# Row-summed modulation coefficients, a reordered opening and eight first feature tiles in a SwiGLU block kernel

## The chip, the cores and the metric

The kernel runs on one core of one Trainium2 chip. The metric is the device time of one execution in microseconds (us), from the first to the last instruction with what the launch puts around them; smaller is better. Five engines work side by side, each through its own instructions in order: TensorE (PE, with its weight loads listed as PEld), VectorE (DVE), ScalarE (ACT), GpSimd (POOL) and SyncE (SP), which here issues the loads.

## The reference, cut to what matters

The whole model is three blocks for 256 tokens of width 1024: a block with two SwiGLU layers and two attentions side by side, then two attention and MLP blocks. The change touches how the first block's modulation is made, and the beginning of its first SwiGLU:

```python
mods = (silu(c) @ w_ada + b_ada).reshape(B, 9, 1024)      # shift, scale, gate for 3 sublayers
n = rmsnorm(h, g_pre[i]) * (1 + scale(i)) + shift(i)
f = (silu(n @ w_gate) * (n @ w_up)) @ w_down              # 1024 -> 2816 -> 1024
h = h + 0.5 * gate(i) * rmsnorm(f, g_post[i])
```

`c` is one vector of 1024 numbers and `w_ada` is 1024 x 9216, so the nine modulation vectors are nine matrix-vector products of 1024 x 1024 each; chunk j of the kernel is the j-th of them (0, 3, 6 shifts; 1, 4, 7 scales; 2, 5, 8 gates).

## The kernel before, in words

All matrix work is done in fp32 split into two parts: a weight tile `raw` of 128 x 1024 is loaded, ACT copies it into a rounded high part `wh` (L489), DVE subtracts to get the low part `wl` (L495, now and then POOL), and TensorE adds three products: high by high, high by low, low by high. The activations are split the same way into `nh` and `nl`.

One list, `plan()`, gives the order of all pieces of the weight stream. `pump_one` takes the next piece: it issues loads up to seven pieces ahead on SP's queue (L435), and puts the split, or for a modulation piece the sum, on ACT and DVE. `pump` keeps a set number of split weights ahead of TensorE. Each engine runs its instructions in the order in which Python wrote them. Small side jobs (`bg`) are generators that `tick` moves one step on after each weight.

The opening (`start_ffn`): x is normed and transposed by TensorE into `yT` (features on partitions). Then comes a loop over the eight k-tiles of the 1024 input features. Before k can be used, `n[0][:, k]` and `n[1][:, k]` need the shift and scale of those 128 features. The piece for them (`ad0`) holds 128 columns of the shift and 128 of the scale; ACT and DVE scale its eight row blocks by silu(c) and add them up (L448, L450: 128 x 256 each, one on ACT and seven on DVE), TensorE sums over the partitions with a column of ones (`reduce_`, 4 instructions), two small DVE operations add the bias and the gain (L1019, L1020), ACT makes `y2` and `nh` (L1023, L1024), DVE makes `nl` (L1028). Then `first(k, 0)` and `first(k, 1)` put the gate and up products of feature tiles 0 to 6 (M0 = 7) into seven PSUM banks, 21 matmuls each (three passes over seven tiles). The eighth bank serves the reductions.

After the loop, seven `swiglu` calls (ACT Silu L914, DVE product L915, ACT and DVE split L918, L919) empty the banks, while TensorE goes on with feature tile 7 in the free bank (`ffn_steps`: 24 matmuls for gate, 24 for up), and from then on with up and down tiles.

The modulation chunks 2 to 8 are spread as pieces over the later stream. A chunk of eight pieces (128 rows x 1024 columns) is summed over row blocks by DVE (L458 for the first piece of a shift or scale, L460 for the others, and with `bz`, a tile with the bias in its first row, for the first piece of a gate). Then `ada_columns` (shifts and scales; 16 TensorE instructions with a column of ones) or `ada_gate` finishes the chunk.

Of the kernel before, what the change touches and what calls it, by code (L numbers as in the profile page):

```python
# [10 lines left out]
F32 = mybir.dt.float32  # L11
# [7 lines left out]
P = 128  # L19
S = 256  # L20
# [41 lines left out]
M0 = 7  # L62
# [45 lines left out]
def plan():  # L108
# [23 lines left out]
    for k in range(2):  # L132
        out += [(("ad0", k, 0), 1024), (("ad0", k, 1), 1024)]
        if k == 0:
            out.append((("s0", 0, 0), M0 * P))
    for k in range(8):
        out.append((("s0", k, 1), M0 * P))
        if k < 6:
            out += [(("ad0", k + 2, 0), 1024), (("ad0", k + 2, 1), 1024)]
        if k < 7:  # L140
            out.append((("s0", k + 1, 0), M0 * P))
# [54 lines left out]
def pack_stream(a):  # L196
# [11 lines left out]
    def piece(key):  # L208
        n = key[0]
        if n == "ad0":  # L210
            _, k, q = key
            w = a["w_ada"][0][512 * q:512 * q + 512]
            w = np.concatenate([w[:, P * k:P * k + P], w[:, D + P * k:D + P * k + P]], axis=1)
        elif n == "s0":
# [5 lines left out]
        elif n == "ada":  # L220
            _, j, k = key
            w = a["w_ada"][0][P * k:P * k + P, 1024 * j:1024 * j + 1024]
# [99 lines left out]
def model_kernel(ctx, tc, x, stream, cols, const, rows, bada, relb, onehot, out):  # L322
# [71 lines left out]
    for i in range(2):  # L394
        nc.sync.dma_start(h[1][:, 512 * i:512 * i + 512], x[tk(1), 512 * i:512 * i + 512])
# [16 lines left out]
    bz = cp.tile([P, D], F32, name="bz")  # L412
    pool.memset(bz, 0.0)
    nc.sync.dma_start(bz[0:1, :], bada[2:3, :])
# [15 lines left out]
    ada_end = {}  # L430
    bg = []

    def load(key, n, off):
        raw = w1k("raw0") if key[0] == "ad0" else rawp.tile([P, RAWC], F32, tag="raw", name="raw")
        nc.sync.dma_start(raw[:, 0:n], stream[off:off + P * n].rearrange("(p w) -> p w", p=P))  # L435
        return raw[:, 0:n]

    def ada_item(key, raw):
        if key[0] == "ad0":
            _, k, q = key  # L440
            if q == 0:
                ada_acc["a"] = w256("ada")
            a = ada_acc["a"]
            for j in range(4):
                c = sc[:, 4 * q + j:4 * q + j + 1]
                r = raw[:, j * 2 * P:(j + 1) * 2 * P]
                if q == 0 and j == 0:
                    act.activation(a, r, AF.Copy, scale=c)  # L448
                else:
                    dve.scalar_tensor_tensor(a, r, c, a, op0=ALU.mult, op1=ALU.add)  # L450
            return
        _, j, k = key
        if k == 0:
            ada_acc[j] = w1k("ada")
        a = ada_acc[j]
        c = sc[:, k:k + 1]
        if k == 0 and j % 3 < 2:
            dve.tensor_scalar(a, raw, c, None, op0=ALU.mult)  # L458
        else:
            dve.scalar_tensor_tensor(a, raw, c, a if k else bz, op0=ALU.mult, op1=ALU.add)  # L460
        if k == 1 and j in (2, 5):
            nc.sync.dma_start(bz[0:1, :], bada[j + 3:j + 4, :])
        if k == 7:
            bg.append(ada_end[j](j, a))
            if j == 4:
                st["lo"] = "dve"
# [3 lines left out]
    def pump_one():  # L470
# [7 lines left out]
        if key[0] in ("ada", "ad0"):  # L478
# [25 lines left out]
    def pump(ahead=None):  # L504
        ahead = st["ahead"] if ahead is None else ahead
        while st["i"] < len(items):
            if items[st["i"]][0][0] not in ("ada", "ad0") and st["w"] >= st["rel"] + ahead + extra():
# [356 lines left out]
    bp1 = cp.tile([P, 72], F32, name="bp1")  # L864
    G = {}

    def ada_columns(j, a):
        for _ in range(4 if j == 3 else 2):
            yield
        ps = bank()  # L870
        for k in range(8):
            mm(ps[:, 2 * k:2 * k + 1], a[:, k * P:(k + 1) * P], ones[:, 0:1], start=(k == 0))
        v = ps.rearrange("p (k two) -> p k two", two=2)[:, 0:8, 0]
        i, sh = j // 3, j % 3 == 0
        if sh:
            dve.tensor_tensor(ac_b[:, i, :], v, cl[:, C_BADA + 8 * j:C_BADA + 8 * j + 8], op=ALU.add)
        else:
            tmp = small(8)
            dve.tensor_tensor(tmp, v, bp1[:, 8 * j:8 * j + 8], op=ALU.add)
            dve.tensor_tensor(ac_a[:, i, :], tmp, cl[:, C_GPRE + 8 * i:C_GPRE + 8 * i + 8], op=ALU.mult)  # L880
# [23 lines left out]

    for j in (3, 4, 6, 7):
        ada_end[j] = ada_columns
    for j in (2, 5, 8):
        ada_end[j] = ada_gate
# [69 lines left out]
    def start_ffn():  # L978
# [3 lines left out]
        dve.tensor_scalar(bp1, cl[:, C_BADA:C_BADA + 72], 1.0, None, op0=ALU.add)  # L982
        ss = [small(2) for _ in range(2)]
        for t in range(2):
            for hf in range(2):
                square_sum(half(t, hf), D, ss[t][:, hf:hf + 1])
        tps = []
        for t in range(2):
            r = inv_rms(ss[t])
            ys = [w512("y") for _ in range(2)]  # L990
            for hf in range(2):
                if t:
                    act.activation(ys[hf], half(t, hf), AF.Copy, scale=r)
                else:
                    dve.tensor_scalar(ys[hf], half(t, hf), r, None, op0=ALU.mult)
            tps += [transposes(ys[hf], 4) for hf in range(2)]
        pump_one()
        pump_one()
        for i, tp in enumerate(tps):
# [971 lines left out]
```

## Time and profile before

| what | us |
|---|---|
| median of 3 runs | 1164.33 (1160.9 to 1165.6) |
| the profiled execution, its own time | 1167.6 |
| its span, first to last instruction | 1165.8 |
| PE busy | 1120.3 |
| DVE busy | 746.2 |
| ACT busy | 603.4 |

The mean granted clock of TensorE in the profiled execution is 0.99. How to read it: an engine's busy time is the union of its instructions, a row of the timeline is a start, a length, the engine, the line, what is written from what, and in brackets how long the engine had been idle and what released it. Matmuls overlap, so the step from one start to the next is the price of one, not its length.

### The profile page before, as it was taken

What the parts mean: (1) busy time and instruction counts of PE and PEld (TensorE: products, weight loads), DVE (VectorE), ACT (ScalarE), POOL (GpSimd) and SP (SyncE); (2) the same over time, 40 slices, a digit from 0 to 9 for tenths busy, and PEclk for the clock granted to TensorE, in tenths of its full rate; (3) what the DMA queues carried; (4) which work ended last, traced back from release to release, by engine and by line L of the source; (5) the groups of instructions that cost most, each with busy time, mean ns of one, the idle gap of its engine ahead of it and who ended that gap; (6) DMA issues with size and microseconds to landing.
All of it is one profiled execution on the core that took longest, in us unless ns stands there. A gap on an engine that the chain in (4) does not pass through costs nothing.

```text
span 1165.8 us, 18854 instructions
## 1 busy us (share of the span) xinstructions
PE 1120.3 (96%) x7268; PEld 1012.5 (87%) x7268; DVE 746.2 (64%) x1286; ACT 603.4 (52%) x1159; POOL 144.4 (12%) x152
## 2 busy tenths in 40 slices
PE   5999999899999899999999799999999999999997
PEld 5998999799888799999887678999998888999996
DVE  5987866689667776455656657555566746655554
ACT  5564444554576544343564566444457655544443
POOL 1001000204000300000058630000003200000001
PEclk9999999999999999999999999999999999999999
DMA  8978977468447385545544234655544523755540
GB/s 289 352 265 318 374 291 244 139 217 325 162 148 250 142 308 190 205 168 184 178 158 149 89 124 143 210 193 188 191 152 140 199 92 126 251 182 184 194 148 37
DMA packets 65920, 230.27 MB, mean 198 GB/s; under 512 B 7275, under 2 KB 8691, under 8 KB 65702
## 3 DMA queue, kind: packets, MB, share of 16 engines
q1 hardware_dynamic: 63798, 225.07, 55.8%
q10 hardware_dynamic: 1776, 3.29, 0.8%
q8 instruction: 57, 0.93, 0.3%
q0 software_dynamic: 256, 0.71, 0.2%
q14 instruction: 33, 0.27, 0.1%
HBM read 227.98 MB, written 2.63 MB: 198 GB/s over the span
## 4 chain that ended last, share of the span: by engine, by line
PE 76%; DVE 10%; ACT 7%; issue 3%; POOL 3%; DMA 0%; SPq 0%; POOLq 0%; ACTq 0%; DVEq 0%
PE mm L547 39%; PE acc L547 35%; DVE wl L495 2%; ACT wh L489 2%; POOL wl L495 2%; PE mm L632 1%; DVE ada L450 1%; DVE ada L460 1%; ACT junk L607 1%; ACT s L1491 1%; POOL sm L604 1%; ACT s L1346 1%; DVE s L1569 0%; DMA h<-in_x_dram 0%; DVE y L701 0%
## 5 line engine op out<-in xcount | busy, mean ns | idle before, releaser
L495 DVE TENSOR_TENSOR wl<-raw,wh 128x1024 fp32r<-128x1024 f32 (+4 forms) x318 | 380.4, 1210 | 86.5 <-ACT wh L489 86.4
L489 ACT ACTIVATE wh<-raw 128x1024 fp32r<-128x1024 f32 (+3 forms) x350 | 354.7, 1034 | 14.0 <-DMA raw<-in_stream_dram 12.9
L547 PE MATMUL mm<-nl,wh 128*128 128x256 f32 x1128 | 314.6, 284 | 0.0
L547 PE MATMUL mm<-nh,wh 128*128 128x256 f32 x1128 | 314.4, 284 | 0.0
L547 PE MATMUL mm<-nh,wl 128*128 128x256 f32 x1128 | 314.3, 283 | 0.0
L547 PEld LDWEIGHTS mm<-nl,wh 128*128 128x128 f32 x1128 | 214.5, 192 | 3.0
L547 PEld LDWEIGHTS mm<-nh,wh 128*128 128x128 f32 x1128 | 214.5, 192 | 3.0
L547 PEld LDWEIGHTS mm<-nh,wl 128*128 128x128 f32 x1128 | 214.2, 192 | 0.0
L547 PE MATMUL acc<-wl,fh 128*128 128x512 f32 x372 | 120.4, 390 | 1.5 <-DVE wl L495 1.5
L547 PE MATMUL acc<-wh,fh 128*128 128x512 f32 x372 | 120.9, 392 | 0.0
L547 PE MATMUL acc<-wh,fl 128*128 128x512 f32 x372 | 119.7, 389 | 0.0
L1089 ACT ACTIVATE rl<-mm 128x256 f32<-128x256 f32 x64 | 24.6, 384 | 160.9 <-PE mm L547 160.9
L495 POOL TENSOR_TENSOR wl<-raw,wh 128x512 fp32r<-128x512 f32 (+2 forms) x64 | 81.7, 1305 | 203.1 <-ACT wh L489 203.1
L604 POOL TENSOR_TENSOR sm<-sm,nhalf 128x1 f32<-128x1 f32 (+1 forms) x36 | 21.5, 597 | 631.4 <-DVE sm L613 566.9
L1090 DVE TENSOR_TENSOR ff<-rl 128x256 f32<-128x256 f32 x64 | 27.2, 425 | 102.5 <-ACT rl L1089 102.5
L914 ACT ACTIVATE sg<-mm 128x256 f32<-128x256 f32 x38 | 14.4, 382 | 137.8 <-PE mm L547 137.8
L547 PEld LDWEIGHTS acc<-wl,fh 128*128 128x128 f32 x372 | 69.9, 188 | 18.1 <-DVE wl L495 3.2
L547 PEld LDWEIGHTS acc<-wh,fl 128*128 128x128 f32 x372 | 69.9, 188 | 14.8
L547 PE MATMUL acc<-wh,nh 128*128 128x512 f32 (+3 forms) x208 | 79.2, 404 | 1.1 <-ACT nh L637 1.1
L547 PE MATMUL acc<-wh,nl 128*128 128x512 f32 (+3 forms) x208 | 75.3, 386 | 0.6 <-DVE nl L638 0.6
L547 PE MATMUL acc<-wl,nh 128*128 128x512 f32 (+3 forms) x208 | 75.1, 385 | 0.0
L547 PEld LDWEIGHTS acc<-wh,fh 128*128 128x128 f32 x372 | 65.5, 189 | 9.1
(322 smaller groups left out, 1638.3 us busy)
## 6 DMA issues: line engine op xcount, KB each, us to landing
raw<-in_stream_dram SPq DMA_DIRECT2D x395, 512.0 KB, 4.6
raw<-in_stream_dram SPq DMA_DIRECT2D x16, 448.0 KB, 6.5
raw<-in_stream_dram SPq DMA_DIRECT2D x8, 384.0 KB, 3.4
raw<-in_stream_dram SPq DMA_DIRECT2D x8, 292.0 KB, 3.2
gp<-in_rows_dram SPq DMA_DIRECT2D x3, 512.0 KB, 6.6
wide<-scr ACTq DMA_DIRECT2D x1, 1536.0 KB, 9.3
raw<-in_stream_dram SPq DMA_DIRECT2D x4, 320.0 KB, 3.0
h<-in_x_dram SPq DMA_DIRECT2D x4, 256.0 KB, 3.6
```

Of the source, the lines that this page charges most:

```text
L450: dve.scalar_tensor_tensor(a, r, c, a, op0=ALU.mult, op1=ALU.add)
L460: dve.scalar_tensor_tensor(a, raw, c, a if k else bz, op0=ALU.mult, op1=ALU.add)
L489: act.activation(wh[:, 0:n], raw, AF.Copy)
L495: e.tensor_tensor(wl[:, u:v], raw[:, u:v], wh[:, u:v].bitcast(F32), op=ALU.subtract)
L547: pe.matmul(o, l, r, start=start, stop=True, skip_group_check=True)
L604: pool.tensor_tensor(o, v, nhalf[:, 0:v.shape[-1]], op=ALU.pow)
L607: act.activation(junk(p_.shape[-1]), p_, AF.Square, scale=1.0 / math.sqrt(n) if scale is None else scale, accum_out=acc_)
L632: pe.transpose(tp[:, j * P:(j + 1) * P], src[:, j * P:(j + 1) * P], ident)
L914: act.activation(sg, ps[:, 0:S], AF.Silu)
L1089: act.activation(rl, ps[:, 0:S], AF.Relu)
L1090: dve.tensor_tensor(ff, rl, rl, op=ALU.mult)
L1346: act.activation(s[:, c], s[:, c], AF.Exp, bias=nm[:, t:t + 1], accum_out=rsum[:, 2 * t + j:2 * t + j + 1])
```

## The change

Shifts and scales (chunks 0, 1, 3, 4, 6, 7) come transposed in the stream: a piece now holds 128 output features on the partitions and all 1024 inputs along the row. silu(c) is spread over all partitions once (`cb`, by eight TensorE instructions against the identity and two ACT operations), and one DVE operation for each piece multiplies and sums along the row, with bias and gain as its scalars, and leaves a finished coefficient column. The TensorE reductions with ones, `ada_columns` and the small DVE operations behind them are gone. Gates keep their sum over row blocks, but their bias now comes in as eight 128 x 128 ACT copies of the identity scaled by the bias; the tile `bz`, its memset and its three small loads are gone.

In the opening, the second half of x is loaded behind the first modulation piece, its squares are summed by DVE, the coefficients for k = 0 are applied straight from PSUM, and the first group of matmuls runs in two halves of four banks. M0 is 8: eight feature tiles run in the k loop, on all eight PSUM banks, and `ffn_steps` starts at tile 8.

```diff
-M0 = 7
+M0 = 8
...
     def ada_item(key, raw):
...
+        if j % 3 < 2:
+            dst, init, scale = (ac_b, cl[:, C_BADA + 8 * j + k:C_BADA + 8 * j + k + 1], 1.0) if j % 3 == 0 else \
+                (ac_a, bpg[:, 8 * i + k:8 * i + k + 1], cl[:, C_GPRE + 8 * i + k:C_GPRE + 8 * i + k + 1])
+            dve.tensor_tensor_reduce(out=raw, in0=raw, in1=cb, scale=scale, scalar=init, op0=ALU.mult, op1=ALU.add,
+                                     accum_out=dst[:, i, k:k + 1])
         else:
-            dve.scalar_tensor_tensor(a, raw, c, a if k else bz, op0=ALU.mult, op1=ALU.add)
...
+            if k == 0:
+                ada_acc[j] = w1k("ada")
+                for m in range(8):
+                    act.activation(ada_acc[j][:, m * P:(m + 1) * P], ident, AF.Copy,
+                                   scale=cl[:, C_BADA + 8 * j + m:C_BADA + 8 * j + m + 1])
+            a = ada_acc[j]
+            dve.scalar_tensor_tensor(a, raw, sc[:, k:k + 1], a, op0=ALU.mult, op1=ALU.add)
...
+        cps = [bank() for _ in range(2)]
+        for k in range(8):
+            mm(cps[k // 4][:, k % 4 * P:k % 4 * P + P], cl[:, C_C + k:C_C + k + 1].broadcast_to([P, P]), ident,
+               start=(k % 4 == 0))
+        raws.append(load(*items[0]))
+        for i in range(2):
+            nc.sync.dma_start(h[1][:, 512 * i:512 * i + 512], x[tk(1), 512 * i:512 * i + 512])
...
+        for i in range(2):
+            act.activation(cb[:, 512 * i:512 * i + 512], cps[i], AF.Silu)
...
+        for hf in range(2):
+            dve.tensor_tensor_reduce(out=ys[1][hf], in0=half(1, hf), in1=half(1, hf), scale=1.0 / D, scalar=0.0,
+                                     op0=ALU.mult, op1=ALU.add, accum_out=ss[1][:, hf:hf + 1])
...
         def coefficients(k):
-            ps = red[0]
...
+            src = yT[:, k, :] if k else tps[0][:, 0:S]
+            a, b = ac_a[:, 0, k:k + 1], ac_b[:, 0, k:k + 1]
+            act.activation(n[0][:, k, :], src, AF.Identity, scale=a, bias=b)
             y2 = w256("y2")
+            act.activation(y2, src, AF.Identity, scale=a, bias=b)
...
+            if k == 0 and q == 0:
+                groups = [((passes[0], passes[2], passes[1]), ms) for ms in (range(4), range(4, M0))]
...
         for k in range(8):
             pump_one()
             first(k, 0)
             if k < 7:
-                reduce_(k + 1)
```

## Rows read from the trace of the kernel before

**Rows 1.** The page: busy time of the engines, share of the span, instructions.
```profile
PE 1120.3 (96%) x7268; PEld 1012.5 (87%) x7268; DVE 746.2 (64%) x1286; ACT 603.4 (52%) x1159; POOL 144.4 (12%) x152
```

**Rows 2.** Timeline of the start: start us, length us, engine, instruction, [idle before, releaser].
```profile
7.87 0.63 ACT L607 ACTIVATE junk<-h 128x512 bf16<-128x512 f32 x1 [1.04 <-DMA h<-in_x_dram]
...
9.51 1.33 ACT L993 ACTIVATE y<-h,sm 128x512 f32<-128x512 f32 x2 [0.92 <-POOL sm L604]
...
11.27 3.68 DVE L450 SCALAR_TENSOR_TENSOR ada<-raw,sc,ada 128x256 f32<-128x256 f32 x7 [2.43 <-ACT ada L448]
...
18.44 1.23 PE L547 MATMUL acc<-nh,wh 128*128 128x256 f32 x4 [2.36 <-ACT wh L489]
```

**Rows 3.** Timeline of VectorE through one turn of the k loop.
```profile
31.38 0.21 DVE L1020 SCALAR_TENSOR_TENSOR ac_a<-mm,bp,cl 128x1 f32<-128x1 f32 x1
...
33.46 0.42 DVE L1028 TENSOR_TENSOR nl<-y,nh 128x256 fp32r<-128x256 f32 x1
...
33.79 2.09 DVE L495 TENSOR_TENSOR wl<-raw,wh 128x896 fp32r<-128x896 f32 x2
...
35.80 1.52 DVE L450 SCALAR_TENSOR_TENSOR ada<-raw,sc,ada 128x256 f32<-128x256 f32 x3
...
37.30 0.21 DVE L1020 SCALAR_TENSOR_TENSOR ac_a<-mm,bp,cl 128x1 f32<-128x1 f32 x1
```

**Rows 4.** Windows of the opening: busy (count) per engine, granted clock, DMA share, GB/s.
```profile
20.00:25.00 5.00, 5.00 (x25) 4.91 (x25) 4.75 (x10) 0.03 (x1) 0.00 (x0) 1.00 0.64 211
25.00:30.00 5.00, 5.00 (x34) 5.00 (x34) 4.89 (x11) 3.10 (x5) 0.00 (x0) 1.00 0.93 337
30.00:35.00 5.00, 5.00 (x44) 4.97 (x43) 4.82 (x12) 3.10 (x5) 0.00 (x0) 1.00 1.02 392
```

**Rows 5.** Timeline where the opening ends: first swiglu, tile 7, first down tile.
```profile
67.84 0.66 ACT L914 ACTIVATE sg<-mm 128x256 f32<-128x256 f32 x2 [2.41 <-PE mm L547]
67.88 0.28 PE L547 MATMUL mm<-nh,wh 128*128 128x256 f32 x1
68.26 0.42 DVE L915 TENSOR_TENSOR sg<-sg,mm 128x256 f32<-128x256 f32 x1 [1.17 <-ACT sg L914]
...
78.63 0.42 DVE L919 TENSOR_TENSOR Fl<-sg,Fh 128x256 fp32r<-128x256 f32 x1
...
79.40 0.63 PE L547 MATMUL acc<-wh,Fh 128*128 128x512 f32 x2
```

**Rows 6.** Timeline of TensorE around the column reduction of chunk 3.
```profile
159.83 1.84 PE L547 MATMUL mm<-onesr,ada 128*128 128x1 f32 x16
161.54 0.70 PE L547 MATMUL acc<-wh,fh 128*128 128x512 f32 x2
```

**Rows 7.** VectorE's multiply-and-reduce: by form (total, mean ns); one line (min/median/max, starts).
```profile
L1341 DVE CUSTOM_DVE_ANT_0 s<-acc,biasT 128x256 f32<-128x256 f32 x8 | 3.3, 418 | 0.0
L1341 DVE CUSTOM_DVE_ANT_0 s<-acc,biasT 128x128 f32<-128x128 f32 x8 | 2.3, 287 | 0.0
...
L1500 DVE CUSTOM_DVE_ANT_0 ljk<-lamin x2: 217/221/225, 573.9 to 574.2; 128x64 f32<-128x64 f32 x2
```

**Rows 8.** Groups by form: busy us, mean ns of one, idle before.
```profile
L489 ACT ACTIVATE wh<-raw 128x1024 fp32r<-128x1024 f32 x318 | 329.2, 1052 | 14.0 <-DMA raw<-in_stream_dram 12.9 <-DMA wide<-scr 1.1
...
L460 DVE SCALAR_TENSOR_TENSOR ada<-raw,sc,ada 128x1024 f32<-128x1024 f32 x49 | 62.8, 1283 | 0.0
...
L448 ACT ACTIVATE ada<-raw,sc 128x256 f32<-128x256 f32 x8 | 4.0, 494 | 0.0
...
L458 DVE TENSOR_SCALAR ada<-raw,sc 128x1024 f32<-128x1024 f32 x4 | 3.0, 748 | 3.8 <-POOL al L890 3.8
```

**Rows 9.** Timeline of the attention stage: gate chunk 5 starts; TensorE waits for scores.
```profile
245.07 1.28 DVE L460 SCALAR_TENSOR_TENSOR ada<-raw,sc,bz 128x1024 f32<-128x1024 f32 x1
...
289.13 0.71 PE L632 MATMUL mm<-kc,s 128*128 128x128 f32 x3 [0.16 <-ACT s L1346]
```

**Rows 10.** Window between the two rows above, columns as in the windows of the opening.
```profile
250.00:255.00 5.00, 5.00 (x44) 4.41 (x42) 5.00 (x9) 2.59 (x5) 0.00 (x0) 1.00 0.88 301
```

More of the change, by code (lines that the diff above doesn't have):

```diff
@@ L321, in model_kernel @@
 @with_exitstack
[L322 removed]
+def model_kernel(ctx, tc, x, stream, cols, const, rows, relb, onehot, out):
     nc = tc.nc
@@ L410, in model_kernel @@
     smaskb = cp.tile([P, P], BF16, name="smaskb")
-    bz = cp.tile([P, D], F32, name="bz")
-    pool.memset(bz, 0.0)
-    nc.sync.dma_start(bz[0:1, :], bada[2:3, :])
+    cb = cp.tile([P, D], F32, name="cb")
     rb = cp.tile([32, 8], F32, name="rb")
@@ L506, in pump @@
         while st["i"] < len(items):
-            if items[st["i"]][0][0] not in ("ada", "ad0") and st["w"] >= st["rel"] + ahead + extra():
+            if items[st["i"]][0][0] != "ada" and st["w"] >= st["rel"] + ahead + extra():
                 if not spare or ahead < NR:
@@ L863, in model_kernel @@
     ac_b = cp.tile([P, 3, 8], F32, name="ac_b")
-    bp1 = cp.tile([P, 72], F32, name="bp1")
+    bpg = cp.tile([P, 24], F32, name="bpg")
     G = {}
[L867 to L880, printed above, removed]
     def ada_gate(j, a):
@@ L981, in start_ffn @@
         yT = big(F32, "yT")
-        dve.tensor_scalar(bp1, cl[:, C_BADA:C_BADA + 72], 1.0, None, op0=ALU.add)
-        ss = [small(2) for _ in range(2)]
[L984 to L996, printed above, removed]
+        dve.scalar_tensor_tensor(bpg.rearrange("p (a b) -> p a b", b=8),
+                                 cl[:, C_BADA:C_BADA + 72].rearrange("p (a b) -> p a b", b=24)[:, :, 8:16], 1.0,
+                                 cl[:, C_GPRE:C_GPRE + 24].rearrange("p (a b) -> p a b", b=8), op0=ALU.add, op1=ALU.mult)
@@ L997, in start_ffn @@
+        r1 = inv_rms(ss[1])
+        for hf in range(2):
+            act.activation(ys[1][hf], half(1, hf), AF.Copy, scale=r1)
         pump_one()
         pump_one()
-        for i, tp in enumerate(tps):
-            act.activation(yT[:, 4 * (i % 2):4 * (i % 2) + 4, tk(i // 2)], tp.rearrange("p (a b) -> p a b", a=4), AF.Copy)
-        acc = [abank() for _ in range(4)] + [bank() for _ in range(M0 - 4)]
-        sums = [ada_acc["a"]]
-        red = [None]
-        def ada_half():
-            pump_one()
-            if sums[-1] is not ada_acc["a"]:
-                sums.append(ada_acc["a"])
@@ L1010, in reduce_ @@
-        def reduce_(k):
-            ps, a = bank(), sums[k]
-            red[0] = ps
-            mm(ps[:, 0:1], a[:, 0:P], ones[:, 0:1], start=True)
-            mm(ps[:, 2:3], a[:, P:2 * P], ones[:, 0:1])
+        tps = [bank() for _ in range(4)]
+        for t in range(2):
+            for k in range(8):
+                pe.transpose(tps[k // 2][:, k % 2 * S + t * P:k % 2 * S + t * P + P],
+                             ys[t][k // 4][:, k % 4 * P:k % 4 * P + P], ident)
         def coefficients(k):
-            ps = red[0]
-            dve.tensor_tensor(ac_b[:, 0, k:k + 1], ps[:, 0:1], cl[:, C_BADA + k:C_BADA + k + 1], op=ALU.add)
-            dve.scalar_tensor_tensor(ac_a[:, 0, k:k + 1], ps[:, 2:3], bp1[:, 8 + k:9 + k], cl[:, C_GPRE + k:C_GPRE + k + 1],
-                                     op0=ALU.add, op1=ALU.mult)
+            src = yT[:, k, :] if k else tps[0][:, 0:S]
+            a, b = ac_a[:, 0, k:k + 1], ac_b[:, 0, k:k + 1]
+            act.activation(n[0][:, k, :], src, AF.Identity, scale=a, bias=b)
```

93 lines of the change are left out of this document (39 added, 54 removed).

## The prediction, made before the result was known

> **What bounds the kernel now.** I read the page first: TensorE is busy 96% of the span, VectorE 64% and ScalarE 52% [rows 1]. So over most of the span only work taken off TensorE, or waits in front of it, can shorten the time, and the places to look at are those where TensorE is not what ends last. Three such places touch this change.
>
> The first is the start. The timeline shows TensorE's first product of the k loop at 18.44 us [rows 2]. Before it stands a chain: the last half of x arrives at 7.87, ACT norms it from 9.51, and only then does VectorE add up the first modulation piece, from 11.27 on for 3.68 us [rows 2]. The second is the k loop. In one turn VectorE goes from its small operation at 31.38 to the same one at 37.30 with work all the way: 5.92 us a turn [rows 3]. TensorE needs less: from 67.88 to 79.40 it runs 96 matmuls of 256 columns, 0.12 us each [rows 5], so 42 of them are 5.04 us and the four reduction instructions 0.43 (a quarter of 1.71, below). VectorE sets the pace of the loop. The third is the attention stage, where VectorE is busy 5.00 of 5.00 us [rows 10] and TensorE already waits a little for its result at 289.13 [rows 9].
>
> Also in the windows: in 20 to 25 us TensorE starts 25 matmuls, in 30 to 35 us 44 [rows 4]. [...] The window between holds 34, so the step falls about 27 us, some 8.6 us after TensorE began to work without pause.
>
> **The change part by part.** The sum is made against the profiled execution, 1167.6 us (span 1165.8), which is 3.3 above the median of the runs.
>
> (a) *Price of the new VectorE operation.* The multiply-and-reduce exists in this trace: 0.418 us for 256 columns, 0.287 for 128 [rows 7], so 1.02 ns a column and 1.20 us for 1024. The accumulator read behind it comes on top: two at line 1500, 64 columns each, start 0.3 us apart [rows 7]; with 960 more columns that is 1.28 us. The sum over row blocks that it replaces takes 1.28 too [rows 8], so in the late chunks VectorE pays the same, save for four first pieces that were cheap at 0.75 [rows 8]. [...] I take 1.28: line 1500 has both operands in SBUF as here, and its 0.221 us lies on the line through the other two (0.287 less 64 times 1.02 ns is 0.222).
>
> [...]
>
> (b) *Start.* On SP's queue one 512 KB piece now stands before the second half of x. At 337 GB/s [rows 4] that is 1.5 us, so x is complete at 9.4 instead of 7.87. Then: squares and sum of a 512-column half on VectorE 0.7 (0.287 plus 384 times 1.02 ns), the steps over VectorE and POOL 0.9 (the idle time before ACT's norm is 0.92), ACT's two norm copies 1.33 [rows 2], the split of the first weight 1.05 [rows 8], the first modulated tile 0.6 (0.494 for a scaled copy of that size [rows 8], plus the bias). 9.4 + 0.7 + 0.9 + 1.33 + 1.05 + 0.6 = 14.0; with hops I take 14.3. The two modulation pieces lie beside this on VectorE (2.6 us from about 10.4). Ends: 13.3, if x isn't held up much, and 16, if the third piece, which must also have landed, comes late. SP's later loads wait for buffers as before.
>
> (c) *The loop.* VectorE per turn: two new operations 2.56, two weight splits of 1024 columns 2.28 (1.005 start to start for 896 columns, plus 128 more), one low part 0.33 [rows 3]: 5.17 us. TensorE: 48 matmuls, 5.76 us, and no reductions. TensorE now sets the pace. ACT has 2 x 1.05 + 2 x 0.6 = 3.3. Loads: 2.10 MB in 5.76 us is 364 GB/s; 392 is reached over 30 to 35 us [rows 4].
>
> All eight tiles are 384 matmuls. I give 42 of them the slow step (8.6 us, as before) and 342 the fast one (41.0): 14.3 + 49.6, plus 0.4 for gaps in the first group, ends at 64.3. Before, tile 7 ended 48 steps after 67.88, at 73.64. **Gain 9.3 us.** Ends: start at 13.3, 10.3; start at 16 with the fast step only from 27 on (4.1 us later than I assume for a start at 14.3, 0.42 lost of each), 5.9.
>
> (d) *No free bank.* Tile 8's first matmul needs a PSUM bank; all eight are full until the first swiglu has read one. Before, Silu began at 67.84 and VectorE's product ended at 68.68 while TensorE went on at 67.88 [rows 5]. Now TensorE waits for it: Silu can start 0.12 earlier, **loss 0.8 us** (0.5 to 1).
>
> (e) *Eight swiglus, and ACT's eight bias copies among them.* Gate chunk 2 begins right behind the first swiglu. Its copies, about 0.3 us start to start (0.494 for twice the columns, less overlap [rows 8]), take 2.4 us; VectorE's first sum waits for the last of them, and behind it in VectorE's queue are the other swiglus. Before, VectorE's part ended at 79.05, TensorE's first down matmul was at 79.40 [rows 5], but that one needs only the first banks. VectorE ends about 2.4 us later (1.7 of waiting, 0.7 for one more tile), TensorE is 0.8 late as well. I book 0.3; ends 0 and 1.5.
>
> (f) *Column reductions of chunks 3, 4, 6, 7.* 16 instructions hold TensorE from 159.83 to 161.54, 1.71 us [rows 6]. Four times that is 6.8. In the attention stage (chunk 6) part may turn into a wait. **Gain 6.3 us**; ends 5.1 (three chunks) and 6.8.
>
> (g) *The attention stage.* The copies of gate chunk 5 come just before its first sum at 245.07 [rows 9] and push VectorE back by about 0.9 us; the first piece of chunk 6 costs 1.28 instead of 0.75, and a few reads add 0.2. VectorE has no gap there [rows 10], and TensorE waits at its end [rows 9]. **Loss 1.6 us**, ends 0 and 2.6. The copies of chunk 8 stand on ACT ahead of weights that TensorE has not come to yet: nothing.
>
> The three loads of the bias row and the memset go; TensorE hides them today.
>
> Sum: -9.3 + 0.8 + 0.3 - 6.3 + 1.6 = -12.9. The profiled execution would be 1154.7, the median 1164.3 - 12.9 = **1151.4 us**. All good ends together give 1147, all bad ends 1158.4.
>
> **The rivals.** *Loads pace the loop.* If loads get only 337 GB/s, as in 25 to 30 us [rows 4], a turn takes 6.2 us; over seven turns 3.2 us go. At 300, 7.0 us a turn and 8.6. Against it stand the 392, and that before, in that window, SP was held back by buffers, not by the memory. Time 1154 to 1160.
>
> [...]
>
> *Slower: the new operation is dearer still.* Its bias and gain come as pointers, two in one operation, and no row here has that together with an accumulator. Each 1 us on its price, once VectorE paces the loop (from 1.8 on), costs 16 us there and 5 in the attention stage. With 1.8 as the point where that begins, 12.9 us are used up at about 2.3 us a piece; from 2.6 on the kernel is over 0.5% slower, at 3.2 about 1180. For it: nothing but the missing row. Against it: the sum at 1.28 that it replaces has a pointer too.
>
> *It doesn't make TensorE start earlier*: x late and the first weight late. Then (c) is worth 5.9 or less, 1155 to 1158; that is in the bounds.
>
> **How the numbers follow.** Forecast with its bounds (1147 to 1158) 0.76; loads pacing 0.12; half speed 0.08; dearer 0.04. 0.5% is 5.8 us, about what can be told from no change. Faster by more than that (below 1158.5): 0.76 + 0.08 of the loads case = 0.84. Within 0.5%: the rest of the loads case and the half-speed case, 0.12. Slower: 0.04. The range for 8 in 10 takes in the bounds and most of the loads case: 1146 to 1160.
>
> **What would show it.** After: first product of the loop near 14.3; VectorE's new operations 1.2 us long; TensorE without gaps from 24 us to the end of the loop near 64, then one gap of 0.8; no matmuls with the column of ones; a wait of 1 to 2 us more near the first scores of the attention stage. I'm wrong if a piece takes over 1.8 us, if ScalarE waits for loads in the loop, or if TensorE's slow step lasts past 27 us.

## The result and the profile after

| | before | after |
|---|---|---|
| median, measured side by side | 1163.37 us (4 runs, 1160.9 to 1165.6) | 1151.04 us (4 runs, 1149.15 to 1151.89) |
| ratio after / before | | 0.9888, 95% interval 0.9866 to 0.9909 |
| profiled execution / its span | 1167.6 / 1165.8 | 1150.4 / 1148.6 |

The forecast was 1151.4. The changed kernel was timed on two more occasions (below). Over all its 16 runs the mean is 1153.4, over 37 runs of the kernel before it is 1164.0: a gain of 10.6 us, where the first four runs gave 12.3 and the sum 12.9.

Between the two profiled spans lie 17.2 us. With the same ScalarE instructions of the two traces set side by side, 12.5 to 13.3 us are won by 400 us of before; the other 4 or so come later and are no effect of the change. About 3 of them come from one VectorE instruction on two columns. It takes 0.22 us in half of its eight places and 5.24 here, and it ends together with GpSimd instructions that stand without a gap from 626.86 to 639.35 (more on this in the last section):

```profile
634.13 5.24 DVE L1566 SCALAR_TENSOR_TENSOR sm<-sm,nlam 128x2 f32<-128x2 f32 x1
```
```profile
626.86 7.54 POOL L495 TENSOR_TENSOR wl<-raw,wh 128x512 fp32r<-128x512 f32 x6
634.35 1.28 POOL L1481 TENSOR_TENSOR ro<-t,t 128x512 f32<-128x512 f32 x1
...
638.07 1.28 POOL L1481 TENSOR_TENSOR ro<-t,t 128x512 f32<-128x512 f32 x1
```

This collision is in nine of the fourteen profiles of this document, at 617 to 634 us, of changed kernels too. In the profile after, the same instruction got through in 0.26 us, and the next two took 2.76 instead of 0.75.

The page of after, the line that answers to [rows 1]: TensorE is busy 12.7 us less and keeps its share.

```profile
PE 1107.6 (96%) x7188; PEld 998.5 (87%) x7188; DVE 741.0 (65%) x1274; ACT 607.7 (53%) x1171; POOL 147.0 (13%) x151
```

The timeline of the start, answering to [rows 2] (columns as there). Line 439 is the new multiply-and-reduce, 533 every matmul, 590 GpSimd's power for the norm:

```profile
8.08 0.69 DVE L973 CUSTOM_DVE_ANT_0 y<-h 128x512 f32<-128x512 f32 x1 [0.18 <-DMA h<-in_x_dram]
...
9.59 1.28 DVE L439 CUSTOM_DVE_ANT_0 raw<-raw,cb,cl 128x1024 f32<-128x1024 f32 x1
9.75 1.52 POOL L590 TENSOR_TENSOR sm<-sm,nhalf 128x1 f32<-128x1 f32 x1 [2.77 <-DVE sm L599]
11.31 1.33 ACT L977 ACTIVATE y<-h,sm 128x512 f32<-128x512 f32 x2 [3.87 <-POOL sm L590]
...
14.10 1.22 PE L533 MATMUL acc<-nh,wh 128*128 128x256 f32 x4
15.12 0.79 PE L533 MATMUL acc<-nh,wl 128*128 128x256 f32 x4
15.75 0.64 PE L533 MATMUL acc<-nl,wh 128*128 128x256 f32 x4
```

The loop's first product stands at 14.10 instead of 18.44. Four matmuls take 1.22 us there and 0.64 (0.12 each, start to start) from 15.75 on. One turn of VectorE in the loop, answering to [rows 3], and two windows, answering to [rows 4]:

```profile
29.36 1.28 DVE L439 CUSTOM_DVE_ANT_0 raw<-raw,cb,cl 128x1024 f32<-128x1024 f32 x1
...
30.56 1.34 DVE L439 CUSTOM_DVE_ANT_0 raw<-raw,cb,bpg 128x1024 f32<-128x1024 f32 x1
...
31.83 0.42 DVE L996 TENSOR_TENSOR nl<-y,nh 128x256 fp32r<-128x256 f32 x1
32.17 2.46 DVE L481 TENSOR_TENSOR wl<-raw,wh 128x1024 fp32r<-128x1024 f32 x2
34.55 1.28 DVE L439 CUSTOM_DVE_ANT_0 raw<-raw,cb,cl 128x1024 f32<-128x1024 f32 x1
```
```profile
25.00:30.00 5.00, 5.00 (x44) 5.00 (x43) 4.63 (x8) 3.11 (x4) 0.00 (x0) 1.00 1.02 405
30.00:35.00 5.00, 5.00 (x44) 5.00 (x43) 4.98 (x8) 3.11 (x4) 0.00 (x0) 1.00 1.02 408
```

VectorE's turn is 5.19 us (29.36 to 34.55), less than TensorE's 5.76 (48 matmuls, 30.14 to 35.90); TensorE is busy all the way and the loads run at 405 to 408 GB/s. ScalarE's splits do wait for loads, up to 1.81 us in this profile, and once TensorE stands for it, 0.70 us; behind that it has no gap to the end of the loop:

```profile
25.44 1.06 ACT L475 ACTIVATE wh<-raw 128x1024 fp32r<-128x1024 f32 x1 [1.81 <-DMA raw<-in_stream_dram]
```
```profile
21.41 0.75 PE L533 MATMUL acc<-nh,wh 128*128 128x256 f32 x4 [0.70 <-ACT wh L475]
```

The end of the loop, answering to [rows 5]:

```profile
61.66 0.38 ACT L880 ACTIVATE sg<-mm 128x256 f32<-128x256 f32 x1 [7.80 <-PE mm L533]
62.08 0.42 DVE L881 TENSOR_TENSOR sg<-sg,mm 128x256 f32<-128x256 f32 x1 [6.74 <-ACT sg L880]
62.55 0.38 PE L533 MATMUL mm<-nh,wh 128*128 128x256 f32 x1 [0.57 <-DVE sg L881]
```

Eight tiles are done at 62.55 less the wait of 0.57, that is 61.98, where the kernel before had them at 73.64. So far 11.7 us are won. No matmul with the column of ones is left in the place of [rows 6]. But where the first SwiGLU's last down product is complete and ACT first reads it, the timelines show 198.55 after and 207.79 before: 9.2 us, although two column reductions, 3.4 us, have gone in between. Something cost 5.9 us. This is where most of it shows: ACT's timeline, then TensorE's, then windows of after (columns as in [rows 4]):

```profile
123.68 0.42 ACT L884 ACTIVATE fh<-sg 128x256 fp32r<-128x256 f32 x1 [13.12 <-PE acc L533]
```
```profile
125.10 0.73 PE L533 MATMUL acc<-wh,fh 128*128 128x512 f32 x2 [1.00 <-ACT wh L475]
127.02 0.74 PE L533 MATMUL acc<-wl,fh 128*128 128x512 f32 x2 [1.18 <-DVE wl L481]
```
```profile
115.00:120.00 5.00, 5.00 (x42) 4.92 (x41) 0.00 (x0) 0.00 (x0) 0.00 (x0) 1.00 0.34 107
120.00:125.00 5.00, 4.10 (x24) 3.26 (x22) 0.79 (x2) 1.32 (x3) 0.00 (x0) 1.00 0.00 0
125.00:130.00 5.00, 3.72 (x11) 2.72 (x12) 5.00 (x7) 3.16 (x5) 0.00 (x0) 0.81 0.87 284
130.00:135.00 5.00, 5.00 (x36) 4.81 (x36) 4.17 (x7) 1.48 (x2) 0.00 (x0) 0.85 0.91 299
```

ACT waits 13.12 us for a matmul, from 110.6 on. In 115 to 120 neither ACT nor VectorE does anything, loading stops, and TensorE lives on weights made earlier; at 124 it has used them up, stands for 2.2 us in two waits, and then works for a while at a lower level of the granted clock. It reads 0.50 from 128.5 to 131.5, where a matmul of 256 columns takes 0.21 to 0.22 us from start to start (130.59 to 131.24), and 1.00 from 132 on, where it takes 0.12. Over 5 us each it is 0.81 and 0.85; by these readings I estimate 0.19 and 0.15 of 5 us lost, 1.7 in all. The kernel before has 4.61 us in the place of the 13.12 and no wait of TensorE there; its row on ACT:

```profile
120.17 0.42 ACT L918 ACTIVATE fh<-sg 128x256 fp32r<-128x256 f32 x1 [4.61 <-PE acc L547]
```

### The profile page after: what moved, and what is told of

Read it like the earlier page. It is cut to its first block, busy times and chain, and to the rows that moved or that the text cites. A ratio compares the mean times of both kernels' runs of the same rounds, so it can differ in the third digit from the quotient of the medians.

```text
span 1148.6 us, 18664 instructions
## 1 busy us (share of the span) xinstructions
PE 1107.6 (96%) x7188; PEld 998.5 (87%) x7188; DVE 741.0 (65%) x1274; ACT 607.7 (53%) x1171; POOL 147.0 (13%) x151
## 4 chain that ended last, share of the span: by engine, by line
PE 78%; DVE 7%; ACT 6%; POOL 4%; issue 3%; DMA 2%; SPq 0%; POOLq 0%; ACTq 0%; DVEq 0%
PE mm L533 38%; PE acc L533 38%; POOL wl L481 2%; DVE wl L481 2%; ACT wh L475 2%; PE mm L618 1%; ACT junk L593 1%; DMA raw<-in_stream_dram 1%; DVE raw L439 1%; ACT s L1466 1%; ACT s L1321 1%; POOL sm L590 1%; DMA h<-in_x_dram 0%; DVE s L1544 0%; DVE y L687 0%
## 5 line engine op out<-in xcount | busy, mean ns | idle before, releaser
L481 DVE TENSOR_TENSOR wl<-raw,wh 128x1024 fp32r<-128x1024 f32 (+1 forms) x316 | 380.8, 1218 | 87.5 <-ACT wh L475 87.2
L533 PE MATMUL acc<-wl,fh 128*128 128x512 f32 (+1 forms) x368 | 119.7, 392 | 3.2 <-DVE wl L481 3.2
L533 PE MATMUL acc<-wh,fh 128*128 128x512 f32 (+1 forms) x368 | 120.1, 393 | 1.0 <-ACT wh L475 1.0
L533 PE MATMUL acc<-wh,fl 128*128 128x512 f32 (+1 forms) x368 | 118.9, 390 | 0.0
L533 PEld LDWEIGHTS acc<-wl,fh 128*128 128x128 f32 x368 | 69.3, 189 | 20.5 <-DVE wl L481 5.7
```

The source lines that it names most:

```text
L481: e.tensor_tensor(wl[:, u:v], raw[:, u:v], wh[:, u:v].bitcast(F32), op=ALU.subtract)
L533: pe.matmul(o, l, r, start=start, stop=True, skip_group_check=True)
```

## The experiments

**The changed kernel again**, for the comparison with the next three.

> The changed kernel once more, as the yardstick for the three runs beside it on the same chip. Every theory: 0.986 to 0.991 of the kernel before, about 1151 us.

1155.01 us (1151.41 to 1158.23, 6 runs), ratio 0.9917, 0.9893 to 0.9941. ACT's wait is again 13.12 us, TensorE's two waits again come to 2.19, but without the lower level behind them. The time lies a little above what I expected. The start came out otherwise: VectorE waits 0.82 us for the second half of x and begins its squares at 8.80 instead of 8.08, and every step up to the first product, at 14.82, is later by as much. The slow step lasts until about 17.9, and the eight tiles are done at 63.42.

**One down tile earlier.** The high and low halves of a SwiGLU tile live in rings of four buffers (lines 361 and 362, NF = 4). Tile m + 4 can't be written before the down product of tile m has read its buffer. With eight tiles in the first part, tile 12 needs tile 8's buffer, and that product stands behind all of the up matmuls of tile 13 in TensorE's order; with seven, tile 11 needs tile 7's, which comes right behind tile 11. Taking one more down tile at up tile 10 frees the buffer sooner:

```
-        for _ in range(0 if m < lead - 1 else 2 if m > start or not start else 0):
+        for _ in range(0 if m < lead - 1 else 3 if start == 8 and m == 10 else 2 if m > start or not start else 0):
```

> The changed kernel with one down tile moved forward: three down tiles instead of two stand behind feature tile 10. In the changed kernel ScalarE waits 13.1 us at its split of tile 12, with VectorE idle behind it, and TensorE then loses 1.0 + 1.2 us and some 0.6 more, with a granted clock of 0.81 and 0.85 from 125 to 135 us. Theory A: the high and low parts of a tile lie in a ring of four buffers, tile 12 needs the buffer of tile 8, and down tile 8 stands on TensorE behind the whole of tile 13; with the ring one down tile earlier the wait falls to about 5 us as in the kernel before, TensorE's gap goes and the time falls by about 4 to 5 us, to 1146. Theory B: the gap comes from loads or from the gate of chunk 2 (its part on GpSimd and the bias table's DMA lie there too); then nothing changes, 1151.

1151.65 us (1149.1 to 1155.63, 6 runs), ratio 0.9885, 0.9862 to 0.9908: 3.4 under the changed kernel beside it by the medians, where theory A said 4 to 5. Its row on ACT and its windows:

```profile
122.70 0.42 ACT L884 ACTIVATE fh<-sg 128x256 fp32r<-128x256 f32 x1 [5.19 <-PE acc L533]
```
```profile
115.00:120.00 5.00, 4.66 (x25) 3.79 (x24) 5.00 (x5) 1.33 (x2) 1.65 (x1) 1.00 0.85 291
120.00:125.00 5.00, 5.00 (x32) 4.49 (x31) 2.92 (x5) 2.30 (x4) 0.00 (x0) 1.00 0.83 261
```

The wait of 13.12 is 5.19, TensorE's idle time there falls from 2.19 to 0.34 (a wait for GpSimd's part of gate chunk 2), and engines and loads go on. Its start was worse in the profile (eight tiles done at 66.2 by ACT's read at 65.89, 2.8 later than in the changed kernel again), and yet it is level with that at 200 us (198.99 against 198.38). The order of the ring was the cause of the stall.

**Seven tiles**, the rest of the change kept (`-M0 = 8`, `+M0 = 7`).

> The changed kernel with seven feature tiles in the opening, as in the kernel before: the first half of the change alone. Theory A: the matmuls of a tile cost the same in the loop and behind it, so the eighth tile brings nothing by itself; without it the wait for a bank (0.7 us) and most of the ring's wait (about 5 us) are gone, as tile 11 needs the buffer of tile 7 whose down tile comes right behind: 1145 to 1147. If loads (1.97 MB in 5.04 us, 390 GB/s) or VectorE (4.9 us a turn) pace the shorter loop a little, 1147 to 1149. Theory B: the gain rests on the eighth tile, which fills TensorE in the loop; then half of the gain or more goes, 1157 or above.

1150.35 us (1144.35 to 1153.3, 6 runs), ratio 0.9873, 0.9846 to 0.9899: 4.7 under the changed kernel beside it by the medians, though above every range of theory A. Theory B is out. No wait for a bank, and TensorE busy 5.00 of 5.00 in all four windows from 115 to 135. The second stage's first read stands at 195.10 where eight tiles have 198.38.

**Seven tiles once more, beside the changed kernel.**

> Seven feature tiles on the changed kernel, a second time. By the account of TensorE's waits in the trace (0.57 us for the tile without a bank and 2.19 us for the ring of four buffers fall away) it stands 2.8 us under the changed kernel; the 4.7 us of the earlier call had in its profiles another 1.7 us from one stretch at half clock more near 220 in the changed kernel, which the theory calls chance. If eight tiles cost all of 4.7, the difference stays at 4 to 5.

> The changed kernel as it is, for the comparison with the three others on one chip: 1151 to 1155 us.

Seven tiles 1152.59 (1147.69 to 1155.83), ratio 0.9902 (0.9878 to 0.9926); the changed kernel 1152.17 (1151.07 to 1157.38), ratio 0.9913 (0.9891 to 0.9935). The medians alone, 4.7 us apart in the first comparison, are level here, so neither my 2.8 nor the 4.7 is confirmed by them. The runs' mean granted clock goes with it: over the 16 runs of the changed kernel the time falls by 0.97 us for each 0.001 of clock, over the 12 runs with seven tiles by 1.03, and the clock goes from 0.987 to 0.997 (over 37 runs of the kernel before the slope is a quarter of that, so the rule is one of these two kernels). Put to a clock of 0.991 at 1.0 us for 0.001, eight tiles give a mean of 1153.0 (standard error 0.5) and seven 1151.0 (0.3). The eighth tile costs 1.9 us, plus or minus 1.2. As they are, the means are 1153.4 and 1151.1, 2.3 apart, plus or minus 2.3. Neither way is clean: in one of three profiles the lower level stands right behind the eighth tile's stall (0.81 and 0.85 in the windows above). If the stall brought it, which isn't shown, setting the clocks equal takes that part of its price away. In the second profiles the stage behind the first SwiGLU is reached at 194.64 with seven and 196.46 with eight, 1.8 apart. So the traces and the times agree that the eighth tile by itself loses about 2 us, and the rest of the change then brings more than the whole.

**The removed reductions put back**, as dead work on a tile that nobody reads: the 16 matmuls with the column of ones for each of chunks 3, 4, 6 and 7, queued as before behind the chunk's last piece.

```
+            if j in (3, 4, 6, 7) and k == 7:
+                bg.append(ones_again(4 if j == 3 else 2))
```

> The changed kernel with the column reductions of chunks 3, 4, 6 and 7 put back as work whose result nobody reads: 16 TensorE instructions with the column of ones and one small VectorE copy for each chunk, at the places where they stood. It measures the step on the reductions by itself. Theory A: each holds TensorE 1.71 us and all four lie on the path, so 6.3 to 6.8 us more than the changed kernel, 1157 to 1158. Theory B: they lay in time in which TensorE waited anyway; then under 2 us, 1151 to 1153.

1160.28 us (1155.21 to 1163.64, 10 runs), ratio 0.996, 0.9941 to 0.9979. Two of its four groups on TensorE, as long as in [rows 6]:

```profile
159.45 1.84 PE L535 MATMUL mm<-onesr,cb 128*128 128x1 f32 x16
...
309.21 1.84 PE L535 MATMUL mm<-onesr,cb 128*128 128x1 f32 x16
```

Its mean (1159.7) is 4.7 us above that of the six runs of the changed kernel beside it and 6.3 above that of all 16; term (f) was 6.3. But the test is not the old state, and the agreement hides two differences. The groups of chunks 3, 6 and 7 stand where they stood before (159.83, 316.10 and 362.71 there; 159.45, 309.21 and 357.44 here), while that of chunk 4 comes at 238.17 instead of 201.68, in the attention stage, where VectorE sets the pace; it costs 0.3 to 1.0 us there, against the profiles of the changed kernel and its variants. And chunk 6's costs more than its own length. These are TensorE's waits for the masked probabilities on both sides of it, before, then after:

```profile
310.54 0.27 PE L547 MATMUL mm<-smaskb,identb 128*128 128x128 bf16 x2 [0.88 <-ACT pT L1354]
...
336.03 0.65 PE L547 MATMUL mm<-smaskb,identb 128*128 128x128 bf16 x4 [1.50 <-ACT aTs L1403]
```
```profile
302.87 0.27 PE L533 MATMUL mm<-smaskb,identb 128*128 128x128 bf16 x2 [0.88 <-ACT pT L1329]
...
324.41 0.65 PE L533 MATMUL mm<-smaskb,identb 128*128 128x128 bf16 x4 [1.50 <-ACT aTs L1378]
```
```profile
310.00:315.00 5.00, 4.46 (x25) 3.96 (x25) 3.02 (x6) 3.29 (x8) 0.00 (x0) 0.66 0.48 174
```

The stretch takes 25.49 us before and 21.54 after. With the group put back it takes 25.60 (305.18 to 330.78), and in the eleven profiles without it 21.5 to 21.6: 4.0 us, of which the group holds TensorE for 1.71. Another 0.47 is a wait that falls away with it, and 1.7, by estimate, a stretch at the lower level (the last row is a window of before, granted clock 0.66, so 0.34 of 5 us; 0.50 in 312 to 314) that all three profiles with the group have and none of the eleven without it. In before it begins ahead of the group, so why the two go together stays open.

**The new operation twice** on the 16 pieces of the opening: a second one of the same operands into a tile that nobody reads, so that a piece costs about 2.6 us.

```
+            if j < 2:
+                dve.tensor_tensor_reduce(out=w512("dup").bitcast(BF16), in0=raw, in1=cb, scale=scale, scalar=init,
+                                         op0=ALU.mult, op1=ALU.add, accum_out=dst[:, i, k:k + 1])
```

> The changed kernel with the multiply-and-reduce of every modulation piece of the opening (16 pieces) done twice, the first time into a scratch tile that nobody reads: the price of a piece doubled to about 2.55 us in the loop alone. Theory A, the rival's arithmetic of the prediction: VectorE then needs 32 x 1.27 + 16 x 1.14 + 8 x 0.33 = 61.5 us from 9.6 on and paces the loop, which ends near 73 instead of 62: about 11 to 12 us more than the changed kernel, no longer faster than the kernel before. Theory B, loads or TensorE hide a dearer piece: under 4 us more.

1167.13 us (1164.27 to 1173.07, 8 runs), ratio 1.0042, 1.0017 to 1.0067. VectorE, then ACT at the end of the loop, then a window:

```profile
29.16 0.42 DVE L999 TENSOR_TENSOR nl<-y,nh 128x256 fp32r<-128x256 f32 x1
...
36.96 0.42 DVE L999 TENSOR_TENSOR nl<-y,nh 128x256 fp32r<-128x256 f32 x1
```
```profile
79.47 0.38 ACT L883 ACTIVATE sg<-mm 128x256 f32<-128x256 f32 x1 [6.14 <-PE mm L536]
```
```profile
50.00:60.00 10.00, 7.77 (x62) 7.24 (x60) 9.89 (x16) 3.00 (x4) 0.00 (x0) 1.00 0.94 336
```

A turn is 7.80 us (29.16 to 36.96), VectorE is busy 9.89 of 10 and TensorE 7.77, and the loop ends 16 to 18 us later. That is more than theory A's 73 for the end of the loop and its 11 to 12 us: VectorE's last activation split of the loop ends at 71.3, about where that sum has it, and TensorE's last 8.5 us of products come behind it. At that price in the opening alone the change is slower than no change. This is the prediction's rival of a dearer operation, made real: it lay at this distance, and the measured 1.28 to 1.34 is what kept it away.

**The order of the first loads.** The second half of x loaded ahead of the first modulation piece:

```
-        raws.append(load(*items[0]))
         for i in range(2):
             nc.sync.dma_start(h[1][:, 512 * i:512 * i + 512], x[tk(1), 512 * i:512 * i + 512])
+        raws.append(load(*items[0]))
```

> The changed kernel with the second half of x loaded ahead of the first modulation piece, as in the kernel before. It tests the step on the start. Theory A: x is complete about 1 us earlier (7.8 instead of 8.7), and the first product of the loop moves from 14.1 to 15.4 (the span of the four executions read so far) to 13 to 14. Theory B: GpSimd's power step in the chain, 1.5 us long beside VectorE's long operations where it takes 0.55 alone, and the first modulation pieces set the start: no move.

1154.76 us (one run). The first product stands at 14.00, beside 14.10, 14.82 and 14.06 in three profiles of the changed kernel. VectorE's squares of the second half start at 8.01 without a wait for x; in the three profiles of the changed kernel they start at 8.08 after a wait of 0.18, at 8.80 after 0.82 and at 8.08 after none. So the piece in front of x costs the start between nothing and 0.8 us by the execution; one run tells no more.

**Without the gate biases**: the gate coefficients lack their bias here, ACT's 24 bias copies are gone, and the first piece of a gate chunk is the cheap one again.

```
-                for m in range(8):
-                    act.activation(ada_acc[j][:, m * P:(m + 1) * P], ident, AF.Copy,
-                                   scale=cl[:, C_BADA + 8 * j + m:C_BADA + 8 * j + m + 1])
+                dve.tensor_scalar(ada_acc[j], raw, sc[:, k:k + 1], None, op0=ALU.mult)
...
-            dve.scalar_tensor_tensor(a, raw, sc[:, k:k + 1], a, op0=ALU.mult, op1=ALU.add)
+            if k:
+                dve.scalar_tensor_tensor(a, raw, sc[:, k:k + 1], a, op0=ALU.mult, op1=ALU.add)
```

> The changed kernel with the bias of the three gates left out: the first piece of a gate is a plain scaling on VectorE, and the eight ScalarE copies in front of it are gone. It tests the step on the attention stage by positions in the trace. Theory A: VectorE's sums of gate chunk 5 no longer wait for the copies, so from the first to the last of the selection's operations it stands 0.9 us or more earlier against TensorE than in the changed kernel. Theory B: the copies were hidden, and nothing moves there. The whole time moves by 1 us or less, which one execution can't tell.

1147.03 us (one run). TensorE at the scores, after, then without the biases:

```profile
280.55 0.71 PE L618 MATMUL mm<-kc,s 128*128 128x128 f32 x3 [1.08 <-ACT s L1321]
281.43 0.71 PE L618 MATMUL mm<-kc,s 128*128 128x128 f32 x3 [0.16 <-ACT s L1321]
```
```profile
277.23 0.72 PE L617 MATMUL mm<-kc,s 128*128 128x128 f32 x3 [0.75 <-ACT s L1320]
278.11 0.71 PE L617 MATMUL mm<-kc,s 128*128 128x128 f32 x3 [0.16 <-ACT s L1320]
```

From the second stage's first read on ACT to TensorE's wait for the masked probabilities it is 102.75 us before (207.79 to 310.54), 104.32 after (198.55 to 302.87), 104.27 and 104.24 in the other two profiles of the changed kernel, and 103.28 here (196.28 to 299.56). These five profiles all have one stretch at the lower level in this stage (in before the granted clock reads 0.50 in 230 to 232, in after 0.56 in 220 to 222); three variants that keep the biases and have none there take 103.5 to 103.6, so only like may be set beside like. So of the 1.5 us that the attention stage loses, ACT's bias copies and the dearer first piece make 1.0.

**Fillers in the kernel before**: 44, 22 and 18 matmuls of a constant in TensorE's waits ahead of the loop.

```
+        fill(44)
...
+        fill(22)
...
+        fill(18)
```

> The kernel before, with matmuls of ones into an unused PSUM bank in the time when TensorE waits ahead of the loop (44 from the start, 22 behind the second half's transposes, 18 behind the first reduction). It tests why the slow step (0.2 us a matmul) lasted 8.6 us in the kernel before and 1 to 4 us in the changed one. Theory A: the work of TensorE ahead of the loop decides; the changed kernel has 16 more instructions there and no gap behind the transposes. Then the loop's first matmuls, at 18.4 us, already step at 0.12. Theory B: the level rises only a set time after the loop itself starts, whatever came ahead: slow until about 27. The time hardly changes either way, since VectorE paces that loop.

1165.82 us (one run). TensorE's rows at the loop's start:

```profile
19.40 0.75 PE L547 MATMUL acc<-nh,wh 128*128 128x256 f32 x4 [0.30 <-ACT wh L489]
19.98 0.52 PE L547 MATMUL mm<-nh,wh 128*128 128x256 f32 x3
...
24.05 0.60 PE L547 MATMUL mm<-onesr,ada 128*128 128x1 f32 x4 [1.87 <-DVE ada L450]
24.51 1.19 PE L547 MATMUL acc<-nh,wh 128*128 128x256 f32 x4
```

With work ahead of them the first products do run at 0.12 to 0.15 us (the first four from 19.40 to 19.98); their row has 0.75 us, that of [rows 2] 1.23. It buys nothing: TensorE comes to VectorE's sums sooner, waits 1.87 us, and the step is slow behind that wait instead, 1.19 us for four. The opening ends at 68.80 by ACT's read, 67.84 before; from the loop's first product that is 49.40 us in both. VectorE paced the old loop, and the slow step lay in its shadow.

**Fillers in the changed kernel**, 18 between the transposes of the two halves of x, with eight tiles and with seven.

```
         for t in range(2):
+            for _ in range(18 * t):
+                mm(fb[:, 0:P], onesr, onesr, start=True)
             for k in range(8):
                 pe.transpose(tps[k // 2][:, k % 2 * S + t * P:k % 2 * S + t * P + P],
```

> The changed kernel with 18 matmuls of a constant put on TensorE between the transposes of the two halves of x, where it stands idle for about 3.5 us (8.6 to 12.1); they are dead work. In the profiled executions of the changed kernel and its variants the opening either has a stretch of about 3.4 us at half the granted clock, with the first product at 14.7 to 15.4 and the first loop products at 0.2 us (changed kernel again, M0 of seven, one down tile earlier), or it has not, with the first product at 14.1 to 14.2 and 0.12 (changed kernel, no gate biases). Theory that the level falls because TensorE has nothing to do in that wait: the granted clock reads 1.00 from 3 to 20, the products take 0.12 us from the first, the first stands at 14.1 to 14.5, and the time is 0 to 1.7 us under that of the changed kernel on this chip. Rival, that the slow first products are a matter of their operands and not of the wait: 0.2 us each until about 17 as before, no gain; were the 18 to run at half level they take 3.6 us, end at 12.2 and delay the transposes by 0.1 to 1 us, loss up to 1 us.

> The same 18 dead matmuls on the kernel with seven feature tiles. By the theory 0 to 1.7 us under the seven tiles alone, so 1148.5 to 1150.5 beside 1150.4 in the earlier call; it would then be the fastest of all. Rival as for eight tiles: no gain, or up to 1 us lost.

Eight tiles 1153.6 (ratio 0.9918, 0.9894 to 0.9941), seven 1152.03 (0.9898, 0.988 to 0.9916): no gain beside the 1152.17 and 1152.59 measured with them, and the seven lie above the 1148.5 to 1150.5 that the theory gave. Windows of the eight tiles with fillers:

```profile
9.00:12.00 3.00, 2.23 (x21) 2.09 (x19) 2.96 (x8) 0.39 (x1) 1.95 (x2) 1.00 1.02 419
12.00:15.00 3.00, 1.87 (x11) 1.45 (x12) 1.52 (x3) 3.00 (x7) 1.65 (x4) 0.80 1.03 418
15.00:18.00 3.00, 3.00 (x16) 3.00 (x16) 3.00 (x7) 2.47 (x5) 0.00 (x0) 0.50 1.04 353
```

The theory misses, and of the rival only the missing gain holds. The fillers ran at 0.12 us each (2.21 us for 18), and the eight transposes behind them took 1.27 us, at a granted clock of 0.95 in 12 to 14; in the second profile of seven tiles, without fillers, they took 1.97 at 0.50. The clock fell all the same, later, to 0.50 in 15 to 18 and 0.57 in 18 to 21, and the first products were slow until 20.5, at 0.21 us each. What decides when it falls stays open; filling most of the wait was not enough.

## Why the prediction was right

The time is right, but step (e) is wrong, and (c) and (f) are too small. Step by step:

- **(a) Price.** 1.28 us a piece assumed; the 24 pieces with one pointer have 1.28 as their median and the 24 with two 1.34, start to start 1.20 to 1.27. That is below the 1.8 from which, by the prediction's estimate, VectorE would have paced the loop. Half speed of the operation, 0.08 in the prediction's chances, is shown by no run: the new operation reads two fp32 tiles of 1024 columns at these 1.28 to 1.34 us, and the sum over row blocks in [rows 8], which reads two fp32 tiles as well, takes 1.28.
- **(b) Start.** 14.3 forecast; 14.10, 14.82 and 14.06 measured. Three terms under it were off and cancel: VectorE's squares start at 8.08 (8.80 in the profile with 14.82), so x was complete by then and not at 9.4; the squares of both halves stand one behind the other, 1.26 us (8.08 to 9.34) and not 0.7; and the steps from their sum to ACT's norm took 1.97 us (9.34 to 11.31) and not 0.9, since GpSimd's power took 1.52.
- **(c) Loop.** The mechanism holds: VectorE's turn 5.19 (5.17 forecast), TensorE paces, loads at 405 GB/s. Mis-sized is the slow step (0.20 us, from 25 starts in 5 us of [rows 4]), 42 matmuls and 8.6 us by the forecast. It lasted until 15.8 to 17.9 in the profiles of the changed kernel, 1.7 to 3.1 us. The eight tiles were done at 61.98, 63.42 and 61.49 instead of 64.3: gain 10.2 to 12.2, forecast 9.3, above the good end of 10.3 in two of the three.
- **(d) Bank.** 0.8 forecast, 0.57 measured, at 62.55 by the row above.
- **(e) Behind the eighth tile.** This step failed. I looked at the eight SwiGLUs between 62 and 76 and booked 0.3, with 1.5 as the end. They cost nothing there: the first down product stands at 74.16 without a wait. The eighth tile's price lies 50 us later, in the ring of four buffers: 2.2 us of standing in all three profiles of the changed kernel, and 1.7 more, by estimate, at the lower level in one of them. The earlier down tile took 1.85 of the 2.2 away, seven tiles all of it.
- **(f) Reductions.** 6.3 forecast, with 6.8 as the good end; the traces show more. Chunks 3, 4 and 7 give 1.7 each, as taken from [rows 6], but chunk 6, of which I thought that part may turn into a wait, gives 4.0: together 9.1. Putting them back cost 4.7 to 6.3 in the run times, with chunk 4's at another place. One cover seems lost: at about 197 TensorE now waits 0.5 us for a weight split of VectorE, where the kernel before has the reduction of chunk 4 a little ahead, at 201.68, and no wait. No run tests this, since that reduction came later when it was put back; the wait was still there.
- **(g) Attention stage.** 1.6 forecast, 1.5 measured (104.3 against 102.75 us), 1.0 of it from the bias copies and the first piece. The wait at the scores grew by 1.08, within the 1 to 2 announced; [rows 10] keeps its answer, VectorE busy 5.00 of 5.00 in 240 to 245.

Added up from the three profiles: -11.3 (b, c), +0.6 (d), +2.2 (ring), +0.6 (lower level, a third of 1.7), +0.5 (split at 197), -9.1 (f), +1.5 (g): -15.0, and about 1.0 us between 62 and 200 for which I found no place, so -14.0. By position the three are indeed 13.3, 13.5 and 15.5 us ahead of the kernel before at its wait at 381 us. Forecast -12.9, measured -12.3 in the first runs and -10.6 over all. Where the rest goes behind 381 us is open; the collision near 620 us, which most profiles of the changed kernel and its variants have, is a candidate that no run tests. The forecast came out because (c) and (f) were each 2 to 3 us too small and (e) 2 to 4 us too small, with opposite signs, and because something behind 381 us took a part back. That is luck. The prediction's good ends add up to 1147.7, not 1147. Of the rivals, loads didn't pace the loop (405 to 408 GB/s). But ScalarE did wait for them, which the prediction had named as a sign of being wrong, and TensorE stood 0.70 us for it in two of the three profiles. Half speed and a still dearer operation fell with (a).

The fastest version by the account above is the change with seven tiles, about 2 us under the changed kernel and 13 under the one before; the seven-tile medians were 1150.35 and 1152.59. Eight tiles with the earlier down tile, 1151.65, can't be told from it.

## What to carry over

When a loop takes one more tile, follow every ring of buffers behind it to the step at which the reused buffer is read, in the order of the engine that reads it: a stage later, an engine that works in order can stand for 13 us while the bound engine eats up its lead. A sum along rows that VectorE makes where it must touch the data anyhow freed the bound engine of its column reductions here; in the loop it was free, because VectorE's turn (5.19 us) stayed under TensorE's (5.76). A test that puts work back measures the old price only if the work lands in its old place: look for it in the trace. For differences under 3 us, look at the runs' granted clock before believing medians, and ask whether the change itself lowers it.

## What the runs showed of the hardware

**Some instructions of GpSimd and VectorE took longer side by side.** The power of one column took 0.55 us at 6.43 and 1.52 at 9.75 us, beside the new operation; and one new operation took 3.42 instead of 1.28 beside GpSimd's subtraction, as these two rows of after show:

```profile
107.78 3.13 POOL L861 TENSOR_TENSOR al<-ada,ah 128x1024 fp32r<-128x1024 f32 x1
```
```profile
108.57 3.42 DVE L439 CUSTOM_DVE_ANT_0 raw<-raw,cb,cl 128x1024 f32<-128x1024 f32 x1
```

The GpSimd row began first and ends at 110.91; the VectorE row ends at 111.99, 1.1 us later, about the new operation's own length. At the start it is the other way round: the new operation begins at 9.59 and ends at 10.87, the power ends at 11.27, 0.4 later. In both pairs the one that began later ended later and took longer than elsewhere; what holds it up isn't shown, nor that it always happens: the second new operation, from 10.79 on, took its usual 1.34 us though the power ran until 11.27. The collision at 634 us looks like the same thing on a larger scale: the VectorE instruction on two columns begins at 634.13, while GpSimd is at work, and ends at 639.37, where GpSimd first pauses. Starting the new operation behind the power instead of ahead of it might bring the start 0.9 us forward, an estimate from 1.52 less 0.55; this wasn't tried.

**The clock's level changes between executions of one kernel.** In the opening the first eight transposes took 1.97 us in two profiles of the changed kernel (after and the third), where the granted clock reads 1.00 from 9 to 18 us, and 1.22 in the second profile with seven tiles, where it reads 0.50 from 12 to 16. In the second profile of the changed kernel it reads 0.50 from 12 to 15. (That its first product is the latest, 14.82, comes from x, not from the clock: the squares begin 0.72 us later.) A slow step goes with both readings: four products take 0.85 us in that second profile (15.84 to 16.69), where the clock reads 0.53 over 15 to 18, and [rows 4] have 0.20 us a step beside 1.00. So a reading of 1.00 didn't mean the fast step, and what made it slow there isn't shown. Over whole runs the mean granted clock went from 0.987 to 0.997, at 1.0 us for each 0.001 (correlation -0.68 for the changed kernel, -0.93 with seven tiles, -0.23 for the kernel before). By the squares of these, the clock goes with most of the scatter with seven tiles, about half with eight and little of it before; which of the two moves the other isn't shown.
